# Branch projections of a decoder block: two-sided banks, with gate products and merging on GpSimd

## The chip, the core and the metric

The kernel runs on one core of a Trainium2 chip. The metric is device microseconds of one execution. Engines are named as in the profile: PE is TensorE (PEld its weight loads), ACT is ScalarE, DVE is VectorE, POOL is GpSimd, SP is SyncE, which issues the loads.

## What is computed

One layer of a decoder block over 256 tokens of width 1024, in float32: a SwiGLU feed-forward part, a token mixer, and a second feed-forward part. The mixer has two branches, attention and a gated spatial MLP, each of width 512. Cut to the part that the change touches:

```
y_attn = attn @ w_branch_attn        # (256, 512) @ (512, 1024)
y_gmlp = gm   @ w_branch_gmlp        # (256, 512) @ (512, 1024)
gates  = sigmoid(n @ w_gate + b_gate)             # (256, 2048)
merged = gates[..., :D] * y_attn + gates[..., D:] * y_gmlp
h = h + merged @ w_out                            # (256, 1024) @ (1024, 1024)
```

## The kernel before

Float32 products are made of a high and a low part of each operand: `split` casts a tensor to the matmul type on ACT (the high part, L199) and subtracts it from the original on DVE (the low part, L200). A product is the sum of high by high, high by low and low by high.

**Two ways to multiply.** `mm3` (L183 to L187) issues the three products one by one, each 256 or 512 columns wide. `by_passes` (L166 to L181) works in a bank with two sides: a wide matmul of 512 columns (`mm_high`, L159) multiplies high weights by high and low activations at once and puts them into the two halves of the bank, and a narrow one of 256 columns (`mm_low`, L164) adds low weights by high activations to the second half. The halves are added later by `collect`: ACT copies the second half to a tile `lo` (L192), and DVE adds the first half to it (L196). All wide products but the last stand ahead of the narrow ones.

**Weights.** Units of 1 MB are loaded in halves to seven `raw` buffers by SP, and split into a ring of four `w` buffers. A unit's split can start when PE has read the unit four before it for the last time. The units that matter here are w51 to w54 (branch weights: attention and gMLP for features 0 to 511, then both for 512 to 1023), w55 to w58 (`w_out`) and w59, w60 (the first of the second feed-forward part).

**Order.** PE and SP keep the order of the code. On ACT, DVE and POOL a scheduler sets the order when the program is built, and each engine then works off its row strictly in order. PSUM has eight banks of 128 x 512, given out in turn, so the tile that is allocated eight places later waits for a bank's last reader.

**Around the change.** The loop at L586 goes over eight blocks f of 128 output features. Before it stand 16 gate blocks (`pgate`, by `by_passes`); they leave `gates` in the tile `mix_a`. Each block of the loop takes one bank `pb`: its left half sums the attention branch, its right half the gMLP branch, both by `mm3` with 256 columns, 24 matmuls in all. DVE multiplies each half by its gates straight out of PSUM (L595, L597), adds the two (L599), and `split` makes the block of `mT` (tiles `mg`) of it. Then `down` (L612) multiplies `mT` by `w_out` into four banks `acch`, in 96 matmuls of 512 columns: first the blocks 0 to 3 of `mT` with w55 and w56, for all four banks in turn; then, bank by bank, the blocks 4 to 7 with w57 and w58. After a bank is done DVE adds it to `h` (L286) and multiplies by the norm's gain (L223, `hg`), and PE transposes the result (L216, tile `tr`). The eight transposes of the first token half stand ahead of the last bank's 12 matmuls.

Of the kernel before, what the change touches and what calls it, by code (L numbers as in the profile page):

```python
# [10 lines left out]
F32 = mybir.dt.float32  # L11
# [7 lines left out]
P = 128  # L19
D = 1024  # L20
S = 256
NT = S // P
DFF = 2816
KB = D // P
# [19 lines left out]
def block_kernel(ctx, tc, t, out):  # L44
    nc = tc.nc
# [5 lines left out]
    tmp = ctx.enter_context(tc.tile_pool(name="tmp", bufs=2))  # L51
# [3 lines left out]
    def bank(name):  # L55
        return psum.tile([P, 512], F32, tag="ps", name=name)
# [94 lines left out]
    def unit(i, ahead=PAIRED):  # L151
        split_to(i + 1 + ahead)
        return parts[i]


    def mm_high(ps, st, both, first, last):


        nc.tensor.matmul(ps, st, both.rearrange("p two n -> p (two n)"), start=first, stop=last)  # L159

    def mm_low(ps, st, both):

        n = both.shape[-1]
        nc.tensor.matmul(ps[:, n:], st, both[:, 0, :], start=False, stop=False)  # L164

    def by_passes(sides, ks=range(KB)):  # L166


        for k in ks:
            if k < KB - 1:  # L170
                for ps, of in sides:
                    (sh, _), both = of(k)
                    mm_high(ps, sh, both, k == 0, False)
        for k in ks:
            for ps, of in sides:
                (_, sl), both = of(k)
                mm_low(ps, sl, both)
        if KB - 1 in ks:
            for ps, of in sides:
                (sh, _), both = of(KB - 1)  # L180
                mm_high(ps, sh, both, False, True)  # L181

    def mm3(ps, st, mv_, first, last):  # L183
        (sh, sl), (mh, ml) = st, mv_
        nc.tensor.matmul(ps, sh, mh, start=first, stop=False)  # L185
        nc.tensor.matmul(ps, sh, ml, start=False, stop=False)  # L186
        nc.tensor.matmul(ps, sl, mh, start=False, stop=last)  # L187

    def collect(to, ps, n=1):

        lo = tmp.tile([P, S], F32, tag="lo", name="lo")
        nc.scalar.copy(lo, ps[:, S:])  # L192
        high = ps[:, :S]
        if n > 1:
            high, lo = (x.rearrange("p (n c) -> p n c", n=n) for x in (high, lo))
        nc.vector.tensor_add(to, high, lo)  # L196

    def split(hi, lo, src):
        nc.scalar.copy(hi, src)  # L199
        nc.vector.tensor_sub(lo, src, hi.bitcast(F32))  # L200

    def alloc_T(name, tags):

        return [act.tile([P, 4, 2, S], F32R, tag=tag, name=f"{name}{c}") for c, tag in enumerate(tags)]

    def both_of(nT, k):
        return nT[k // 4][:, k % 4]

    def block_of(nT, k):
        return both_of(nT, k)[:, 0, :], both_of(nT, k)[:, 1, :]  # L210
# [44 lines left out]
    def weights_of(w, nT, blk):  # L255
        c = slice(blk * P, (blk + 1) * P)
        return lambda k: ((w[:, k, 0, c], w[:, k, 1, c]), both_of(nT, k))

    def by_weights(name, i, nT, blk):

        ps, w = bank(name), unit(i, ALONE)
        by_passes([(ps, weights_of(w, nT, blk))])
        return ps

    def by_tokens(name, i, nT, j):

        ps, w = bank(name), unit(i)
        tk = slice(j * P, (j + 1) * P)
        by_passes([(ps, lambda k: (tuple(p[:, tk] for p in block_of(nT, k)), w[:, k]))])
        return ps  # L270
# [66 lines left out]
    def ffn_blocks(i0, aT, nT, rows, name, fs):  # L337
        for f in fs:
            gu = tmp.tile([P, 2, S], F32, tag="gu", name=f"gu{name}{f}")
            w = unit(i0 + f, ALONE)  # L340
            ps = [bank(f"{name}{'gu'[i]}{f}") for i in range(2)]
            by_passes([(ps[i], weights_of(w, nT, i)) for i in range(2)])
            for i in range(2):
                collect(gu[:, i, :], ps[i])
            gate_up(aT, gu, rows, name, f)
# [11 lines left out]
    for k, end in zip(CUTS, CUTS[1:]):  # L357
# [9 lines left out]
        for i in range(2):  # L367
            w = parts[i]
# [6 lines left out]
    for group in ((0, 1), (2,), (3,)):  # L375
        at = [(f, i) for f in group for i in range(2)]
        w = {f: unit(f1 + f, PAIRED if len(group) > 1 else ALONE) for f in group}
        ps = {(f, i): bank(f"f1_{f}{i}") for f, i in at}
        sides = [(ps[f, i], weights_of(w[f], nT, i)) for f, i in at]
# [60 lines left out]
    gates = mix_a[:, :2 * KB, :]  # L440
# [43 lines left out]
    for f in range(4):  # L484
        us = tmp.tile([P, S], F32, tag="us", name=f"uz{f}")
# [5 lines left out]
    for j in range(NT):  # L491
        n = (j + 1) * P
# [3 lines left out]
        for a0 in range(0, HEADS // 2, per):  # L496
# [7 lines left out]
            for two in range(2):  # L504
                ps = pair[two].rearrange("p (a n) -> p a n", a=per)
# [26 lines left out]
    aoT, gmT = alloc_T("ag", ("nC", "nD"))  # L532
# [52 lines left out]
    mT = alloc_T("mg", ("nA", "nB"))  # L585
    for f in range(KB):  # L586
        i = mb + 2 * (f // 4)
        ps = bank(f"pb{f}")
        c = slice(f % 4 * P, (f % 4 + 1) * P)
        for q, bT in enumerate((aoT, gmT)):  # L590
            w = unit(i + q)
            for k in range(4):
                mm3(ps[:, q * S:(q + 1) * S], (w[:, k, 0, c], w[:, k, 1, c]), block_of([bT], k), k == 0, k == 3)
        m0 = tmp.tile([P, S], F32, tag="s", name=f"m0{f}")
        nc.vector.tensor_mul(m0, ps[:, :S], gates[:, f, :])  # L595
        m1 = tmp.tile([P, S], F32, tag="us", name=f"m1{f}")
        nc.vector.tensor_mul(m1, ps[:, S:], gates[:, KB + f, :])  # L597
        m2 = tmp.tile([P, S], F32, tag="a", name=f"m2{f}")
        nc.vector.tensor_add(m2, m0, m1)  # L599
        split(*block_of(mT, f), m2)  # L600

    nT3 = alloc_T("n3", ("nC", "nD"))
# [19 lines left out]
    for j in range(NT):  # L622
        s = tmp.tile([P, UC], F32, tag="s", name=f"s{j}")
# [13 lines left out]
    ms, o = {}, {}  # L637
# [93 lines left out]
```

## Time and profile before

| | us |
|---|---|
| median of three runs (lowest, highest) | 542.71 (542.49, 543.24) |
| the profiled execution | 542.64 |
| its span, first to last instruction | 540.9 |
| PE busy | 532.1 |
| DVE busy | 390.7 |
| ACT busy | 303.2 |
| POOL busy | 10.9 |

The profiled execution is 1.74 us longer than its span, and 0.07 us under the median. The mean granted TensorE clock is 0.997 of full speed. Matmul records overlap, since they are pipelined: what one costs is the distance from its start to the next one's start, not its duration. On ACT and DVE, too, the next instruction starts a little before the one ahead of it has ended.

### The profile page before, as it was taken

The page shows a single profiled execution, that of the slowest core. Times are in us where ns is not written, and L with a number is a line of the kernel's source. Part 1 is how long each engine was busy: PE and PEld are TensorE (multiplying, and loading weights), DVE is VectorE, ACT ScalarE, POOL GpSimd, SP SyncE. Part 2 cuts the span into 40 slices and gives each one's busy share as a digit, 9 for nine tenths or more (in the row PEclk, how much of TensorE's full clock was granted, in tenths as well). Part 3 has the DMA queues.
Part 4 walks back from the last instruction along what each step waited for, and adds up shares of the span by engine and source line. Part 5 has one row for each costly group of instructions (what it writes and reads, how often), then busy time and mean ns, then how long its engine had stood idle before and what let it go on. Part 6 is the DMA issues. An engine that isn't in the chain of part 4 may idle for free.

```text
span 540.9 us, 7971 instructions
## 1 busy us (share of the span) xinstructions
PE 532.1 (98%) x2988; PEld 460.8 (85%) x2988; DVE 390.7 (72%) x632; ACT 303.2 (56%) x541; POOL 10.9 (2%) x23
## 2 busy tenths in 40 slices
PE   8999999999999999999999999999999999999995
PEld 6888888888888888888888998888888888888884
DVE  5989978787434676978896687687787877855324
ACT  6886565565424467457966544575565656543302
POOL 0000000000100010000000000000000000000002
PEclk9999999999999999999999999999999999999998
DMA  8977665657755458464275445466655556465002
GB/s 288 416 276 246 219 214 170 209 180 240 247 194 195 156 196 270 160 226 142 77 215 174 148 154 184 162 210 221 206 180 189 200 180 208 164 219 174 32 0 78
DMA packets 29285, 103.02 MB, mean 190 GB/s; under 512 B 3392, under 2 KB 3904, under 8 KB 29248
## 3 DMA queue, kind: packets, MB, share of 16 engines
q1 hardware_dynamic: 29104, 102.33, 56.6%
q8 instruction: 23, 0.38, 0.3%
q10 hardware_dynamic: 144, 0.20, 0.1%
q14 instruction: 14, 0.11, 0.1%
HBM read 101.46 MB, written 1.05 MB: 190 GB/s over the span
## 4 chain that ended last, share of the span: by engine, by line
PE 96%; DMA 1%; DVE 0%; SPq 0%; ACT 0%; issue 0%; POOLq 0%; DVEq 0%; POOL 0%; ACTq 0%
PE acch L185 9%; PE acch L186 9%; PE acch L187 9%; PE f2u L159 7%; PE f2g L159 7%; PE f1u L159 6%; PE f1g L159 6%; PE pgate L159 6%; PE f2u L164 4%; PE f2g L164 4%; PE f L159 3%; PE f1u L164 3%; PE f1g L164 3%; PE pgate L164 3%; PE pq L159 3%; PE f L164 2%
## 5 line engine op out<-in xcount | busy, mean ns | idle before, releaser
L200 DVE TENSOR_TENSOR w<-raw,w 128x1024 fp32r<-128x1024 f32 x180 | 216.8, 1220 | 57.2 <-ACT w L199 56.5
L199 ACT CAST w<-raw 128x1024 fp32r<-128x1024 f32 x180 | 181.5, 1055 | 59.0 <-PE acch L187 39.6
L159 PE MATMUL f2g<-n,w 128*128 128x512 f32 x160 | 62.7, 392 | 0.0
L159 PE MATMUL f2u<-n,w 128*128 128x512 f32 x160 | 62.6, 392 | 0.0
L159 PE MATMUL f1u<-n,w 128*128 128x512 f32 x144 | 56.4, 391 | 0.0
L159 PE MATMUL f1g<-n,w 128*128 128x512 f32 x144 | 56.4, 391 | 0.0
L164 PE MATMUL f2u<-n,w 128*128 128x256 f32 x160 | 39.3, 283 | 0.0
L164 PE MATMUL f2g<-n,w 128*128 128x256 f32 x160 | 39.1, 283 | 0.0
L164 PE MATMUL f1u<-n,w 128*128 128x256 f32 x144 | 35.3, 284 | 0.0
L164 PE MATMUL f1g<-n,w 128*128 128x256 f32 x144 | 35.2, 283 | 0.0
L159 PEld LDWEIGHTS f2u<-n,w 128*128 128x128 f32 x160 | 30.2, 189 | 5.7
L159 PEld LDWEIGHTS f2g<-n,w 128*128 128x128 f32 x160 | 30.2, 188 | 5.5
L159 PE MATMUL pgate<-n,w 128*128 128x512 f32 x128 | 34.7, 400 | 0.0
L185 PE MATMUL acch<-w,f1h 128*128 128x512 f32 x88 | 34.4, 390 | 0.0
L186 PE MATMUL acch<-w,f1h 128*128 128x512 f32 x88 | 34.3, 390 | 0.0
L187 PE MATMUL acch<-w,f1l 128*128 128x512 f32 x88 | 34.3, 390 | 0.0
L186 PE MATMUL acch<-w,f2h 128*128 128x512 f32 x84 | 32.7, 390 | 0.0
L187 PE MATMUL acch<-w,f2l 128*128 128x512 f32 x84 | 32.7, 390 | 0.0
L185 PE MATMUL acch<-w,f2h 128*128 128x512 f32 x84 | 32.7, 390 | 0.0
L159 PEld LDWEIGHTS f1u<-n,w 128*128 128x128 f32 x144 | 27.1, 189 | 5.1
L159 PEld LDWEIGHTS f1g<-n,w 128*128 128x128 f32 x144 | 27.1, 188 | 5.0
L164 PEld LDWEIGHTS f2u<-n,w 128*128 128x128 f32 x160 | 30.7, 192 | 0.8
(194 smaller groups left out, 989.8 us busy)
## 6 DMA issues: line engine op xcount, KB each, us to landing
raw<-in_f SPq DMA_DIRECT2D x84, 512.0 KB, 4.8
raw<-in_f1d SPq DMA_DIRECT2D x22, 512.0 KB, 4.5
raw<-in_f2d SPq DMA_DIRECT2D x22, 512.0 KB, 4.1
raw<-in_gate SPq DMA_DIRECT2D x16, 512.0 KB, 4.1
raw<-in_qk SPq DMA_DIRECT2D x8, 512.0 KB, 4.9
raw<-in_out SPq DMA_DIRECT2D x8, 512.0 KB, 4.1
raw<-in_v SPq DMA_DIRECT2D x4, 512.0 KB, 4.6
raw<-in_gv SPq DMA_DIRECT2D x4, 512.0 KB, 4.5
```

The source lines that it names most:

```text
L159: nc.tensor.matmul(ps, st, both.rearrange("p two n -> p (two n)"), start=first, stop=last)
L164: nc.tensor.matmul(ps[:, n:], st, both[:, 0, :], start=False, stop=False)
L185: nc.tensor.matmul(ps, sh, mh, start=first, stop=False)
L186: nc.tensor.matmul(ps, sh, ml, start=False, stop=False)
L187: nc.tensor.matmul(ps, sl, mh, start=False, stop=last)
L199: nc.scalar.copy(hi, src)
L200: nc.vector.tensor_sub(lo, src, hi.bitcast(F32))
```

## The change

Each block takes two banks, `pb{f}0` for attention and `pb{f}1` for gMLP. In each, `by_passes` with four k steps sums one branch: three wide matmuls, four narrow ones, the last wide one, the two branches alternating. `collect` (ACT copy, DVE add) brings each bank into an SBUF tile `z`; POOL multiplies each `z` by its gates and adds the two, and `split` follows as before.

```diff
-    def by_passes(sides, ks=range(KB)):
+    def by_passes(sides, ks=range(KB), n=KB):
         for k in ks:
-            if k < KB - 1:
+            if k < n - 1:
                 for ps, of in sides:
                     (sh, _), both = of(k)
                     mm_high(ps, sh, both, k == 0, False)
...
-        if KB - 1 in ks:
+        if n - 1 in ks:
             for ps, of in sides:
-                (sh, _), both = of(KB - 1)
+                (sh, _), both = of(n - 1)
                 mm_high(ps, sh, both, False, True)
...
     for f in range(KB):
         i = mb + 2 * (f // 4)
-        ps = bank(f"pb{f}")
         c = slice(f % 4 * P, (f % 4 + 1) * P)
-        for q, bT in enumerate((aoT, gmT)):
+        pb = [bank(f"pb{f}{q}") for q in range(2)]
+
+        def part_of(q, bT):
             w = unit(i + q)
-            for k in range(4):
-                mm3(ps[:, q * S:(q + 1) * S], (w[:, k, 0, c], w[:, k, 1, c]), block_of([bT], k), k == 0, k == 3)
-        m0 = tmp.tile([P, S], F32, tag="s", name=f"m0{f}")
-        nc.vector.tensor_mul(m0, ps[:, :S], gates[:, f, :])
-        m1 = tmp.tile([P, S], F32, tag="us", name=f"m1{f}")
-        nc.vector.tensor_mul(m1, ps[:, S:], gates[:, KB + f, :])
+            return lambda k: ((w[:, k, 0, c], w[:, k, 1, c]), both_of([bT], k))
+
+        by_passes([(pb[q], part_of(q, bT)) for q, bT in enumerate((aoT, gmT))], range(4), 4)
+        ms = []
+        for q in range(2):
+            z = tmp.tile([P, S], F32, tag=("s", "us")[q], name=f"z{q}{f}")
+            collect(z, pb[q])
+            nc.gpsimd.tensor_mul(z, z, gates[:, q * KB + f, :])
+            ms.append(z)
         m2 = tmp.tile([P, S], F32, tag="a", name=f"m2{f}")
-        nc.vector.tensor_add(m2, m0, m1)
+        nc.gpsimd.tensor_add(m2, *ms)
         split(*block_of(mT, f), m2)
```

Three places in the engines' rows show what moves. On PE, block 4 before: the attention half of its 24 matmuls (`ag0` holds the attention branch, w53 its weights).

```order
L185 MATMUL pb4_3241<-ag0_2536,w53_3038 128x256
L186 MATMUL pb4_3241<-ag0_2536,w53_3038 128x256
L187 MATMUL pb4_3241<-ag0_2536,w53_3038 128x256
L185 MATMUL pb4_3241<-ag0_2536,w53_3038 128x256
L186 MATMUL pb4_3241<-ag0_2536,w53_3038 128x256
L187 MATMUL pb4_3241<-ag0_2536,w53_3038 128x256
...
L187 MATMUL pb4_3241<-ag0_2536,w53_3038 128x256
L185 MATMUL pb4_3241<-ag1_2537,w54_3113 128x256
```

The same place of PE in the changed kernel: the wide ones of both branches, then narrow ones, then the last two wide ones.

```order
L159 MATMUL pb40_3237<-ag0_2536,w53_3038 128x512
L159 MATMUL pb41_3238<-ag1_2537,w54_3102 128x512
L159 MATMUL pb40_3237<-ag0_2536,w53_3038 128x512
...
L159 MATMUL pb41_3238<-ag1_2537,w54_3102 128x512
L164 MATMUL pb40_3237<-ag0_2536,w53_3038 128x256
L164 MATMUL pb41_3238<-ag1_2537,w54_3102 128x256
...
L164 MATMUL pb41_3238<-ag1_2537,w54_3102 128x256
L159 MATMUL pb40_3237<-ag0_2536,w53_3038 128x512
L159 MATMUL pb41_3238<-ag1_2537,w54_3102 128x512
```

A block has 8 wide and 8 narrow matmuls now, in place of 24 narrow ones, and both branches end together. On ACT, before, the rows from the cast of block 2 (`m22`) to the first cast of w58:

```order
L199 CAST mg0_3098<-m22_3204 128x256
L199 CAST w55_3242<-raw55_0_2897 128x1024
L199 CAST w55_3242<-raw55_1_2967 128x1024
L199 CAST w56_3263<-raw56_0_2971 128x1024
L199 CAST w56_3263<-raw56_1_3041 128x1024
L199 CAST mg0_3098<-m23_3237 128x256
L199 CAST mg1_3099<-m24_3288 128x256
L199 CAST mg1_3099<-m25_3321 128x256
L199 CAST w57_3397<-raw57_0_3045 128x1024
L199 CAST mg1_3099<-m26_3354 128x256
L199 CAST w57_3397<-raw57_1_3116 128x1024
L199 CAST w58_3430<-raw58_0_3120 128x1024
```

The changed kernel on ACT, from the copies of block 3 to the cast of block 4 (`pb40` is block 4, attention):

```order
L192 COPY lo_3224<-pb30_3205 128x256
L192 COPY lo_3229<-pb31_3206 128x256
L199 CAST w55_3239<-raw55_0_2897 128x1024
L199 CAST w55_3239<-raw55_1_2967 128x1024
L199 CAST mg0_3098<-m23_3233 128x256
L199 CAST w56_3248<-raw56_0_2971 128x1024
L199 CAST w56_3248<-raw56_1_3041 128x1024
L192 COPY lo_3274<-pb40_3237 128x256
L192 COPY lo_3279<-pb41_3238 128x256
L192 COPY lo_3306<-pb50_3287 128x256
L192 COPY lo_3311<-pb51_3288 128x256
L199 CAST mg1_3099<-m24_3283 128x256
```

And the rows of ACT that follow these, up to the casts of w58:

```order
L192 COPY lo_3338<-pb60_3319 128x256
L192 COPY lo_3343<-pb61_3320 128x256
L199 CAST mg1_3099<-m25_3315 128x256
L199 CAST mg1_3099<-m26_3347 128x256
L192 COPY lo_3370<-pb70_3351 128x256
L192 COPY lo_3375<-pb71_3352 128x256
L199 CAST w57_3389<-raw57_0_3045 128x1024
L199 CAST w57_3389<-raw57_1_3105 128x1024
L199 CAST mg1_3099<-m27_3379 128x256
L199 CAST w58_3422<-raw58_0_3109 128x1024
L199 CAST w58_3422<-raw58_1_3242 128x1024
```

Sixteen copies are new on ACT, the cast of block 3 now stands between w55 and w56 with the copies of blocks 4 and 5 behind w56, and the casts of w57 stand behind those of blocks 5 and 6 and the copies of block 7. POOL's row gets 24 instructions, three for each block in order. On DVE the two adds of each block take the place of the two products and the sum, and the subtractions of w56 stand ahead of the adds of block 4.

## Rows read from the trace of the kernel before

**Rows 1.** Page, part 1: busy time, share of the span, instructions.
```profile
PE 532.1 (98%) x2988; PEld 460.8 (85%) x2988; DVE 390.7 (72%) x632; ACT 303.2 (56%) x541; POOL 10.9 (2%) x23
```

**Rows 2.** Waits of PE in the whole span: total us, times, longest.
```profile
PE warm L93 <- DVE zeros L90: 1.2, 1, 1.2
PE f L159 <- ACT w L199: 1.1, 2, 0.8
```

**Rows 3.** Chain that ended last, in order of time: start us, us, what.
```profile
290.69 1.84 PE pgate L159 x8
292.53 0.95 PE pgate L164 x8
```

**Rows 4.** Timeline of PE: start, us, what.
```profile
304.56 0.28 PE L185 MATMUL pb<-ag,w 128*128 128x256 f32 x1
...
327.60 0.40 PE L185 MATMUL acch<-w,mg 128*128 128x512 f32 x1
...
338.50 0.39 PE L185 MATMUL acch<-w,mg 128*128 128x512 f32 x1
...
346.67 1.03 PE L216 MATMUL tr<-ident,hg 128*128 128x128 f32 x8
...
371.82 0.28 PE L164 MATMUL f2g<-n,w 128*128 128x256 f32 x1
...
377.39 0.28 PE L164 MATMUL f2g<-n,w 128*128 128x256 f32 x1
```

**Rows 5.** Timeline of ACT, with idle time before and its releaser.
```profile
304.81 0.37 ACT L192 COPY lo<-pgate 128x256 f32<-128x256 f32 x1 [1.33 <-PE pgate L159]
305.08 2.00 ACT L199 CAST w<-raw 128x1024 fp32r<-128x1024 f32 x2
...
314.64 0.41 ACT L199 CAST mg<-m 128x256 fp32r<-128x256 f32 x1 [2.47 <-DVE m L599]
314.96 3.89 ACT L199 CAST w<-raw 128x1024 fp32r<-128x1024 f32 x4
```

**Rows 6.** Timeline of DVE.
```profile
306.16 2.36 DVE L200 TENSOR_TENSOR w<-raw,w 128x1024 fp32r<-128x1024 f32 x2
308.44 0.42 DVE L595 TENSOR_TENSOR m<-pb,mix_a 128x256 f32<-128x256 f32 x1
...
319.31 1.22 DVE L200 TENSOR_TENSOR w<-raw,w 128x1024 fp32r<-128x1024 f32 x1
320.44 0.42 DVE L200 TENSOR_TENSOR mg<-m,mg 128x256 fp32r<-128x256 f32 x1
...
332.56 1.22 DVE L200 TENSOR_TENSOR w<-raw,w 128x1024 fp32r<-128x1024 f32 x1
...
342.11 0.69 DVE L286 SCALAR_TENSOR_TENSOR h<-acch,h 128x512 f32<-128x512 f32 x1
...
344.87 0.69 DVE L223 TENSOR_TENSOR hg<-h,gain 128x512 f32<-128x512 f32 x1
```

**Rows 7.** Groups of POOL: count, busy us, mean ns, idle before.
```profile
L664 POOL TENSOR_TENSOR o<-o,rstd 128x512 f32<-128x512 f32 x1 | 1.0, 1041 | 0.1
L656 POOL TENSOR_TENSOR ms<-ss,eps 128x1 f32<-128x1 f32 x2 | 0.4, 190 | 173.2 <-ACT sq L652 173.2
```

**Rows 8.** Instructions on the tile rstd: least, median, greatest ns.
```profile
L243 POOL TENSOR_TENSOR rstd<-ms,nhalf x6: 548/548/1463, 26.8 to 354.7; 128x1 f32<-128x1 f32 x6
```

**Rows 9.** Timelines of DVE and POOL around 194 us.
```profile
194.31 0.15 DVE L241 TENSOR_SCALAR ms<-ms 128x1 f32<-128x1 f32 x1
194.38 1.21 DVE L200 TENSOR_TENSOR w<-raw,w 128x1024 fp32r<-128x1024 f32 x1
...
194.54 1.46 POOL L243 TENSOR_TENSOR rstd<-ms,nhalf 128x1 f32<-128x1 f32 x1 [7.98 <-DVE ms L241]
```

**Rows 10.** Busy us (x instructions) by stretch: PE, PEld, DVE, ACT, POOL; clock, DMA.
```profile
304.50:327.60 23.10, 23.10 (x194) 23.06 (x194) 17.93 (x36) 10.12 (x16) 0.00 (x0) 1.00 0.44 149
```

## Prediction

> **What bounds the kernel now.** I read the page's busy times first: PE is busy for 98% of the span [rows 1]. Its list of waits says how much of the rest a change could win: 2.3 us in all, both waits in the first stage, none after it [rows 2]. So PE is the bound from then on, and a change pays what it takes off PE's own row, as long as no other engine becomes late. The busy table by stretch shows the stage: in 23.1 us PE never pauses, DVE works 17.9 us, ACT 10.1, POOL not at all [rows 10]. The timeline of PE gives its ends: the first branch matmul starts at 304.56 and the first of `w_out` at 327.60, which is 23.04 us for 192 matmuls, 0.120 each [rows 4].
>
> **PE's term.** The matmuls that replace them are in the trace already. In a gate block, eight wide ones take 1.84 us (0.230 each) and eight narrow ones 0.95 [rows 3]: 2.79 for a block of the new form, 22.32 for eight. The blocks of the second feed-forward part alternate two banks as the new ones do, with twice the k steps: one starts its narrow matmuls at 371.82, the next at 377.39 [rows 4], so half of one is 2.785, eight 22.28. I take 2.785: the stage is 0.76 us shorter. The bounds are a wide one at 0.227, as in `w_out` (48 from 327.60 to 338.50 [rows 4]), with a narrow one at 0.119, and a wide one at twice a narrow one's 0.120, which gains nothing: 0.9 to 0 us.
>
> **What is added, and its cover.** Sixteen ACT copies of 0.37 us; per block, two DVE adds of 0.42 replace two products and a sum of the same length; 24 POOL instructions. By busy time all this fits: ACT comes to 16 of 22.3 us, DVE to 15. But a block now passes ACT, DVE, POOL and ACT again before its copy is done, and ACT's row is strict: a cast that waits for POOL holds up the copies and the weight casts behind it. So I walked the rows of the four engines in order, each instruction starting when its engine is free and what it reads is there, with these durations. ACT starts the next instruction 0.27 after a copy (304.81 to 305.08), 0.32 after a cast of a block (314.64 to 314.96), 0.95 after a weight cast (four in 3.89) [rows 5]. DVE goes on 1.13 after a weight subtraction (319.31 to 320.44) [rows 6], 0.33 after an add. An engine starts 0.03 after the end of what it waits for, POOL after 0.08 (194.46 to 194.54 [rows 9]); I take 0.12. Walked in the same way, the rows of before give 342.06 for the first `h` add, which the trace has at 342.11 [rows 6], so the method holds to a tenth.
>
> **POOL's price.** No row has this instruction. The same operation takes 1.04 us on 512 columns and 0.19 on one [rows 7]. The straight line between gives 0.615 for 256; half of the long one is 0.52, the floor, and the whole 1.04 is the ceiling. With a fixed part somewhat under 0.19 it is 0.59. I take 0.60, since the same operation at twice the width is the nearest row; its second operand was one column repeated, which the new ones are not, and that is the weak point.
>
> **DVE and POOL in each other's way.** The small power on POOL takes 0.55 us, once 1.46 [rows 8]. That once it started at 194.54 while DVE subtracted a weight half, from 194.38 to 195.59, and it ended at 196.00, 0.41 after DVE [rows 9]: it did most of its work behind the subtraction. The Trainium skill says why, in "SBUF — State Buffer", section "Who interferes with whom": a DVE instruction with both inputs in SBUF and a GpSimd one that reads SBUF exclude each other; this row agrees. In the walk POOL's reading, from 0.14 after its start, and DVE's weight and block subtractions exclude each other, and whoever starts first goes first. The new adds have one input in PSUM and are left free.
>
> **The walk.** Block f is ready at 304.56 + 2.785(f+1) + 0.17, block 0 at 307.51. DVE is busy with w54 until 308.44, as before [rows 6]. From then on the copies of one block, its adds, three POOL steps and its cast take about 1.37 + 3 x 0.60 = 3.17 us, more than PE's 2.785; ACT's order lets no copy of blocks 1 to 3 pass the cast ahead of it. So ACT reaches block 3's copies at 317.49, 1.6 us after the block. Behind them stand w55's casts, block 3's cast (321.21, its sum having waited for a subtraction of w55), w56's casts, and only then block 4's copies (323.43).
> - First deadline: `down` takes the banks of blocks 4 and 5, as the eighth tiles after them; before, those of blocks 0 to 3, long free. PE arrives at 304.56 + 22.28 = 326.84; DVE has emptied the first bank at 325.29. In hand: 1.5 us.
> - Second: ACT waits for POOL with the casts of blocks 4, 5 and 6 (327.26, 329.29, 331.32), then copies block 7 and casts w57 from 332.18, waits for block 7 (335.36), and casts w58. DVE ends w58's second half at 339.11, where before it was done at 333.78 [rows 6]. PE needs it after 57 matmuls of `down`: 326.84 + 57 x 0.227 = 339.8. In hand: 0.7.
> - Third: w59 and w60 occupy DVE until 343.6; then come two `h` adds with two gains, done at 346.27. Before, the last of these ended at 345.56, for transposes at 346.67 [rows 4, 6]. Now the four transposes that need it are due at 346.40. In hand: 0.1.
>
> At 0.60 no wait reaches PE. Later weights have several us in hand.
>
> **The sum.** 542.64 for the profiled execution (540.9 of span and 1.74 around it) - 0.76 = 541.9; it lay 0.07 under the median of 542.71, so the median comes to 542.0. That is 0.14%, inside the 0.2% that a measurement of this kernel can tell from no change.
>
> **What POOL's price does to it.** With the exclusion, 0.615 makes the last transposes wait 0.25: -0.5 us. At 0.65 w58 is 0.5 late too: +0.3. At 0.67 `down` begins to wait for its first bank, which pushes DVE's subtractions behind POOL's reads once more, and w58 is 2.8 late: +3.0. At 0.70: +3.6; at 0.73: +4.3; at the ceiling of 1.04: +11.7. Without the exclusion: -0.76 up to 0.68, +0.1 at 0.73, +7.6 at 1.04.
>
> **The rivals.**
> - *POOL is slower on two full tiles, and the mixer waits for it* (slower). The place is the start of `down` and w58; it decides from 0.66 us per POOL instruction on. For it: the row of 0.60 rests on a repeated column, and the walk's margins are tenths. Against: an instruction would have to be a tenth over the line between the two rows. At 0.67 to 0.74 it gives +3.0 to +4.5, 545.6 to 547.1.
> - The Trainium skill's "GPSIMD Engine Reference", section 3.1, speaks for this rival: 4497 ns for such an addition of 2048 columns, about 2.6 cycles an element. My estimate from that page, its slope on the 0.19 us of one column, is 0.73 us for 256 columns, and the sum would be 546.9. The row of 512 columns goes against it: that rate would have made it 1.27, not 1.04; but no row has two full operands.
> - *The copies never matter, and the wide matmuls run as in* `w_out`, with later waits on PE's sequencer gone too: over 1.09 us of gain, under 541.6. For it only the spread of the runs and the 0.9 above; PE has no other idle time to give back here [rows 2, 10].
> - *Nothing happens*: the new matmuls cost as much per column as the old ones, because the banks alternate; 542.7. The feed-forward blocks alternate and have the low price [rows 4].
>
> **How the numbers follow.** No or hardly a wait on PE, 541.7 to 542.5: 0.46, with 0.08 of that for gains that measure as more than 0.2%. A short wait or no gain, to 543.7: 0.17. The mixer waits for POOL, 543.8 to 546.6: 0.27; above that 0.10. So faster 0.08, same 0.55, slower 0.37. The predicted time is that of the first case. The range leaves out the tenth above, and something below 541.7: 541.7 to 546.6. The likeliest case alone: 541.7 to 542.5.
>
> **What the profile after would show.** PE's term: 128 `pb` matmuls, a block each 2.79 us, 22.3 from the first to `down`. POOL's price: the spacing of its 24 instructions; 0.60 is right, 0.70 is the rival. The lag: ACT's copies of block 4 at about 323.4, after w56's casts. Margins: no wait of PE on DVE between 326 and 350; the rival shows a gap before the first `acch` matmul, another before w58, and a third before the transposes. Exclusion: POOL's sum of block 3 stretched or late by a subtraction of w55. I would be wrong through POOL's duration first, and through the walk's margins second.

## The result, and the profile after

The changed kernel takes 548.24 us (median of 5 runs, 547.86 to 548.79); the kernel before, on the same chip, 542.98 (5 runs, 542.49 to 543.78). The ratio is 1.0098, with an interval of 1.0087 to 1.0109: 5.3 us slower (4.7 to 5.9). The prediction was 542.0, with a range of 541.7 to 546.6. The profiled execution took 548.13, with a span of 546.4, which is 5.5 over the span before.

The page's busy times of the changed kernel, and its chain that ended last by engine, to be read beside [rows 1]:

```profile
PE 535.1 (98%) x2924; PEld 459.1 (84%) x2924; DVE 388.8 (71%) x624; ACT 307.5 (56%) x557; POOL 33.0 (6%) x47
PE 90%; POOL 3%; DVE 2%; issue 2%; ACT 1%; DMA 1%; POOLq 0%; DVEq 0%; ACTq 0%
```

The shares alone mislead. PE is still busy for 98%, POOL for only 6%. But POOL now has 3% of the chain, 16 us: it has become part of what sets the end. The waits of PE of the changed kernel, which answer to [rows 2], say where that happens (total us, times, longest):

```profile
PE acch L185 <- ACT w L199: 1.2, 1, 1.2
PE warm L93 <- DVE zeros L90: 1.2, 1, 1.2
PE acch L185 <- DVE z L196: 0.9, 1, 0.9
PE acch L186 <- DVE w L200: 0.8, 1, 0.8
PE f L159 <- ACT w L199: 0.6, 1, 0.6
```

Three waits of the matmuls of `down` are new. The timeline of PE in the changed kernel puts them in time, as in [rows 4]:

```profile
304.93 1.54 PE L159 MATMUL pb<-ag,w 128*128 128x512 f32 x6
...
326.82 0.63 PE L159 MATMUL pb<-ag,w 128*128 128x512 f32 x2
328.31 0.50 PE L185 MATMUL acch<-w,mg 128*128 128x512 f32 x1 [0.86 <-DVE z L196]
...
340.62 0.40 PE L187 MATMUL acch<-w,mg 128*128 128x512 f32 x1
342.26 0.50 PE L185 MATMUL acch<-w,mg 128*128 128x512 f32 x1 [1.24 <-ACT w L199]
343.52 0.60 PE L186 MATMUL acch<-w,mg 128*128 128x512 f32 x1 [0.76 <-DVE w L200]
343.92 0.63 PE L187 MATMUL acch<-w,mg 128*128 128x512 f32 x1
...
347.29 0.39 PE L186 MATMUL acch<-w,mg 128*128 128x512 f32 x1
...
351.86 1.03 PE L216 MATMUL tr<-ident,hg 128*128 128x128 f32 x8
```

Read the distances of starts. From the first branch matmul to the first of `down` it is 23.38 us, against 23.04 before: PE's own work is shorter, and the wait for the bank costs 1.03. From there to the transposes it is 23.55, against 19.07: 4.48 more. Of these, 1.41 and 1.03 are the two stops for the last unit of `w_out` (1.64 and 1.26 less the 0.23 that a matmul takes anyhow). Another 1.73 is not a wait at all: from 343.52 to 347.29 nine matmuls start 0.42 us apart on average, which makes 3.77 us, where 9 x 0.227 is 2.04. The remaining 0.3 are matmuls next to a stop that stand up to 0.34 apart instead of 0.23. Together the two stretches are 4.8 us longer; 0.37 more lay ahead of the stage in this execution, 0.3 behind it.

The busy table of the changed kernel by stretch says what the slow matmuls are (columns as in [rows 10]):

```profile
304.90:327.30 22.40, 22.40 (x129) 19.47 (x127) 12.22 (x20) 10.90 (x22) 10.57 (x12) 1.00 0.33 111
328.40:340.60 12.20, 12.20 (x53) 9.89 (x54) 6.61 (x12) 4.85 (x11) 10.58 (x12) 1.00 0.31 100
340.60:343.50 2.90, 0.92 (x3) 0.19 (x1) 1.69 (x3) 2.65 (x4) 0.22 (x1) 1.00 0.80 249
343.50:347.30 3.80, 3.78 (x10) 2.75 (x11) 3.80 (x4) 3.44 (x4) 0.00 (x0) 0.55 0.60 179
```

The granted clock is 1.00 up to 343.50 and 0.55 in the 3.8 us behind it: TensorE ran nearly all of them at the lower of its two levels, 1.2 GHz. Ahead of that PE had worked 0.92 of 2.90 us. The single stop at 327 to 328 did not lower it: the row behind it has 1.00. All this is read from the one profiled execution. The mean granted clock of the five executions is 0.993 (the profiled one), 0.995, 0.996, 0.993 and 0.996, where the 56 executions of the kernel before in the experiments have 0.996 to 0.999; whether all five had the slow stretch is not shown.

Why POOL is in the chain stands in its groups in the changed kernel, which answer to [rows 7]:

```profile
L600 POOL TENSOR_TENSOR z<-z,mix_a 128x256 f32<-128x256 f32 x16 | 13.9, 890 | 92.7 <-DVE z L196 92.7
L603 POOL TENSOR_TENSOR m<-z,z 128x256 f32<-128x256 f32 x8 | 7.6, 951 | 0.6
```

The two means hide two cases. The least, median and greatest ns of the same two groups:

```profile
L600 POOL TENSOR_TENSOR z<-z,mix_a x16: 730/740/1775, 309.3 to 337.4; 128x256 f32<-128x256 f32 x16
L603 POOL TENSOR_TENSOR m<-z,z x8: 732/736/1601, 310.8 to 339.2; 128x256 f32<-128x256 f32 x8
```

An instruction that nothing holds up costs about 0.735 us (medians of 740 and 736 ns), not 0.60, and some last 1.6 to 1.8. The timeline of POOL in the changed kernel shows which:

```profile
312.88 1.43 POOL L600 TENSOR_TENSOR z<-z,mix_a 128x256 f32<-128x256 f32 x2 [1.31 <-DVE z L196]
...
316.43 1.43 POOL L600 TENSOR_TENSOR z<-z,mix_a 128x256 f32<-128x256 f32 x2 [1.31 <-DVE z L196]
...
319.98 2.47 POOL L600 TENSOR_TENSOR z<-z,mix_a 128x256 f32<-128x256 f32 x2 [1.31 <-DVE z L196]
322.53 1.60 POOL L603 TENSOR_TENSOR m<-z,z 128x256 f32<-128x256 f32 x1
```

The timeline of DVE has the first of these rows beside the last two, and the second where block 4's first add stands:

```profile
320.63 2.90 DVE L200 TENSOR_TENSOR w<-raw,w 128x1024 fp32r<-128x1024 f32 x2 [0.40 <-ACT w L199]
...
327.84 0.75 DVE L196 TENSOR_TENSOR z<-pb,lo 128x256 f32<-128x256 f32 x2
```

POOL's loop comes round every 3.55 us (312.88 to 316.43), while PE makes a block in 2.79. And block 3's second product and its sum, which meet the two subtractions of w55, take 1.0 and 0.9 us longer than their fellows; the subtractions take 2.90 instead of the 2.36 of a pair left alone [rows 6].

How that reaches PE is read on ACT, which works off its row strictly in order. Its timeline in the changed kernel:

```profile
318.71 0.41 ACT L199 CAST mg<-m 128x256 fp32r<-128x256 f32 x1 [2.60 <-POOL m L603]
...
324.17 0.41 ACT L199 CAST mg<-m 128x256 fp32r<-128x256 f32 x1 [2.62 <-POOL m L603]
324.48 2.00 ACT L199 CAST w<-raw 128x1024 fp32r<-128x1024 f32 x2
326.37 0.64 ACT L192 COPY lo<-pb 128x256 f32<-128x256 f32 x2
...
340.85 0.40 ACT L199 CAST mg<-m 128x256 fp32r<-128x256 f32 x1 [2.62 <-POOL m L603]
341.17 5.78 ACT L199 CAST w<-raw 128x1024 fp32r<-128x1024 f32 x6
```

Block 4 is copied at 326.37 (the walk had 323.4 at a price of 0.60), and DVE adds it from 327.84, behind the subtractions of w56; so the bank that `down` wants first comes free too late, and its first matmul starts at 328.31. Block 7's cast waits until 340.85, and the casts of w58, the first of the six at 341.17, stand behind it: PE wants that unit at 340.9. Both stops there are for the first half of w58, at the 55th and 56th matmul of `down`; the walk had set its deadline by the second half, after 57.

### The profile page after: what moved, and what is told of

Read it like the earlier page. It is cut to its first block, busy times and chain, and to the rows that moved or that the text cites. A ratio compares the mean times of both kernels' runs of the same rounds, so it can differ in the third digit from the quotient of the medians.

```text
span 546.4 us, 7894 instructions
## 1 busy us (share of the span) xinstructions
PE 535.1 (98%) x2924; PEld 459.1 (84%) x2924; DVE 388.8 (71%) x624; ACT 307.5 (56%) x557; POOL 33.0 (6%) x47
## 4 chain that ended last, share of the span: by engine, by line
PE 90%; POOL 3%; DVE 2%; issue 2%; ACT 1%; DMA 1%; POOLq 0%; DVEq 0%; ACTq 0%
PE acch L186 8%; PE acch L187 8%; PE acch L185 8%; PE f2u L159 7%; PE f2g L159 7%; PE f1u L159 6%; PE f1g L159 6%; PE pgate L159 6%; PE f L159 4%; PE f2u L164 4%; PE f2g L164 3%; PE f1u L164 3%; PE f1g L164 3%; PE pgate L164 3%; PE pq L159 3%; PE f L164 2%
```

## The experiments

All are compared with runs of the kernel before on the same chip: median 542.74 for the matmuls alone, for products and sum on VectorE, for one column repeated in all three, and for GpSimd's part alone; 542.92 for one input tile on VectorE; 542.72 for the other four.

| | us | ratio to before |
|---|---|---|
| the matmuls alone | 541.99 | 0.9986 (0.9977 to 0.9995) |
| products and sum on VectorE | 541.72 | 0.9980 (0.9972 to 0.9989) |
| one column repeated, all three | 542.53 | 0.9998 (0.9989 to 1.0007) |
| products repeated | 543.54 | 1.0013 (1.0004 to 1.0022) |
| sum repeated | 546.83 | 1.0070 (1.0056 to 1.0084) |
| GpSimd's part alone | 547.37 | 1.0086 (1.0072 to 1.0100) |
| last unit early | 546.70 | 1.0070 (1.0056 to 1.0083) |
| only the sum on GpSimd | 541.97 | 0.9984 (0.9975 to 0.9993) |
| one input tile on VectorE | 545.21 | 1.0041 (1.0026 to 1.0055) |

The theory: the matmuls win their 0.76 us, and the 24 GpSimd instructions make ACT late for two deadlines of `down`, because each costs 0.735 us and because GpSimd and VectorE's subtractions with two input tiles keep each other out (called the exclusion below). The first rival: the loss lies in the matmuls, the second bank or ACT's copies. The second: the exclusion plays no part.

### The two halves of the change apart

The kernel before with the new matmuls; VectorE multiplies straight from the first half of each bank, and the second halves are left out:

```diff
-        nc.vector.tensor_mul(m0, ps[:, :S], gates[:, f, :])
+        nc.vector.tensor_mul(m0, pb[0][:, :S], gates[:, f, :])
...
-        nc.vector.tensor_mul(m1, ps[:, S:], gates[:, KB + f, :])
+        nc.vector.tensor_mul(m1, pb[1][:, :S], gates[:, KB + f, :])
```

> The new matmuls in two banks, with DVE multiplying the first half of each bank straight out of PSUM and adding the two, as before; the second halves are left out, and with them the copies, the adds and GpSimd. Theory 1 (GpSimd's price at 0.735 us and its exclusion with DVE stall the mixer): PE's term alone is left, so 0.76 us faster than before, 22.3 us from the first branch matmul to the first of w_out, no wait of PE after the first stage. Theory 2 (the new order of matmuls or the two banks make PE or the banks late): still slower than before by several us.

Measured: 0.75 us faster. Its timeline of PE:

```profile
304.64 1.54 PE L159 MATMUL pb<-ag,w 128*128 128x512 f32 x6
...
327.00 0.39 PE L185 MATMUL acch<-w,mg 128*128 128x512 f32 x1
...
346.06 1.03 PE L216 MATMUL tr<-ident,hg 128*128 128x128 f32 x8
```

22.36 us from the first branch matmul to `down`, 19.06 from there to the transposes: PE's term stands, and in this stage no wait takes anything back.

The other half alone: the matmuls of before in one bank, which ACT copies for POOL:

```diff
-        nc.vector.tensor_mul(m0, ps[:, :S], gates[:, f, :])
...
-        nc.vector.tensor_mul(m1, ps[:, S:], gates[:, KB + f, :])
+            nc.scalar.copy(z, ps[:, q * S:(q + 1) * S])
+            nc.gpsimd.tensor_mul(z, z, gates[:, q * KB + f, :])
...
-        nc.vector.tensor_add(m2, m0, m1)
+        nc.gpsimd.tensor_add(m2, *ms)
```

> The kernel before with its 24 matmuls a block in one bank, but ACT copies both halves of the bank to SBUF and GpSimd multiplies and adds; no DVE adds. Theory 1: the stall comes with GpSimd, without the new matmuls: the walk gives a wait of about 3.2 us before the second half of w58 and 0.6 at the transposes, together 3.8 us slower than before, and up to 2 more if the clock falls behind the gap as in the changed kernel. Theory 2: no slower than before by more than the copies, that is within 0.5 us.

Measured: 4.6 us slower, most of the loss without one new matmul. Its waits of PE:

```profile
PE acch L185 <- ACT w L199: 2.0, 1, 2.0
PE acch L186 <- DVE w L200: 0.8, 1, 0.8
```

And its busy table behind the second of them:

```profile
343.50:347.30 3.80, 3.47 (x9) 2.76 (x10) 3.80 (x5) 2.81 (x3) 0.00 (x0) 0.55 0.57 186
```

The same unit is late, and the clock falls again behind the stops, for as long. The bank of `down` is in time here: its first matmul comes 23.04 us after the first branch matmul, as before, since a block takes one bank.

### The same copies and adds, but on VectorE

```diff
-            nc.gpsimd.tensor_mul(z, z, gates[:, q * KB + f, :])
+            nc.vector.tensor_mul(z, z, gates[:, q * KB + f, :])
...
-        nc.gpsimd.tensor_add(m2, *ms)
+        nc.vector.tensor_add(m2, *ms)
```

> The changed kernel with products and sum on DVE; all else as changed. Theory 1: the walk through the rows, with 0.42 us for each of the three, has DVE done with the second half of w58 at 335.5 and no wait of PE: 0.76 us faster than before, about 542.1. Theory 2 (the additional pass through ACT copies and DVE adds is what comes too late, whoever multiplies): slower than before by 2 us or more, with a gap of PE before w58.

Measured: 1.02 us faster, the best of all kernels here. The second bank, the copies on ACT and the adds cost nothing here, which speaks against the first rival. One caution: the scheduler gives ACT another row in this kernel, where the first copy of block 1 (309.84 us) stands ahead of the cast of block 0 (310.11). That the row alone isn't the cause is shown below by the kernels that keep the changed kernel's row. VectorE has the room: in its busy table it works 20.2 of the 22.4 us, and PE never pauses.

```profile
304.20:326.60 22.40, 22.40 (x130) 19.71 (x129) 20.18 (x44) 12.56 (x27) 0.00 (x0) 1.00 0.47 147
```

With the products on VectorE and only the sum on GpSimd:

```diff
-            nc.gpsimd.tensor_mul(z, z, gates[:, q * KB + f, :])
+            nc.vector.tensor_mul(z, z, gates[:, q * KB + f, :])
```

> The products on VectorE, only the sum of each block on GpSimd, at 0.735 us. A block's chain then takes 0.3 us more than with all of it on VectorE, and no wait reaches TensorE by the walk: -0.8 us like the version with all of it on VectorE (-1.0 measured there). If one GpSimd instruction a block is enough to disturb VectorE's subtractions by the exclusion (0.6 us each time), some tenths come back at most, -0.5. If it is any use of GpSimd that costs, it lies above 0.

Measured: 0.75 us faster. Its sums last 0.73 to 0.79, but one 1.59, and no wait reaches PE. One GpSimd step a block is free here, so it is not any use of the engine that costs. ACT's row is again another than that of the changed kernel.

### The price, in four steps

Four kernels, the changed one among them, have one and the same order of instructions on ACT, DVE and POOL in this stage, and differ in GpSimd's second operands alone. First, all three instructions of a block with a repeated column:

```diff
-            nc.gpsimd.tensor_mul(z, z, gates[:, q * KB + f, :])
+            nc.gpsimd.tensor_mul(z, z, gates[:, q * KB + f, 0:1].to_broadcast([P, S]))
...
-        nc.gpsimd.tensor_add(m2, *ms)
+        nc.gpsimd.tensor_add(m2, ms[0], ms[1][:, 0:1].to_broadcast([P, S]))
```

> The changed kernel, with every row of instructions the same, but the second operand of each GpSimd product and of the sum is one column repeated 256 times, so the values are others. Theory 1, and the reason given for its wrong price (a repeated column is cheaper than a full tile): GpSimd takes 0.59 to 0.615 us for one that no DVE subtraction holds up, and the walk gives 0.76 to 0.5 us faster than before. If the pattern of the operand does not matter: 0.735 us each and 5 us slower than before, as the changed kernel.

Measured: 0.21 us faster, which the interval doesn't tell from no change. The least, median and greatest ns of its products and sums:

```profile
L600 POOL TENSOR_TENSOR z<-z,mix_a x16: 612/613/841, 309.0 to 333.3; 128x256 f32<-128x256 f32 x16
L603 POOL TENSOR_TENSOR m<-z,z x8: 612/612/1474, 310.2 to 334.0; 128x256 f32<-128x256 f32 x8
```

Two rows of ACT's timeline, the copies of block 4 and the cast of block 7:

```profile
323.49 0.64 ACT L192 COPY lo<-pb 128x256 f32<-128x256 f32 x2
...
335.52 0.41 ACT L199 CAST mg<-m 128x256 fp32r<-128x256 f32 x1 [1.20 <-POOL m L603]
```

And its first transposes on PE's timeline:

```profile
345.99 1.26 PE L216 MATMUL tr<-ident,hg 128*128 128x128 f32 x8
```

The price is that of the straight line in the prediction, 0.615, to 3 ns, and the time that the prediction gave for it, -0.5, is 0.3 off. The walk at 0.60 had these two rows of ACT at 323.43 and 335.36. The eight transposes take 1.26 instead of 1.03: the third deadline is missed by 0.23, where the walk had 0.25. The changed kernel's own row of instructions loses nothing at this price; so its loss comes with the price.

Then only the sum repeated (the second edit alone), and only the products (the first alone):

> Leaves out the true sum: the second operand of GpSimd's sum is one column repeated, the two products keep their full tiles; the order of all instructions is that of the changed kernel. Two thirds of GpSimd's instructions then cost 0.735 us, a third 0.613: 0.69 on average. If the loss is a matter of deadlines that GpSimd's steps miss together with the exclusion between VectorE's two-input subtractions and GpSimd, the walk gives a wait of 0.6 at the first matmul of down and of 2.9 at its last unit, +3.4 us, and up to 1.7 more if the clock falls again behind the second: +3.4 to +5.1. If the two engines did not exclude each other, the rows alone give -0.8. If the loss grew evenly with the price (from -0.2 at 0.613 to +5.3 at 0.735), it would be two thirds of the way: +3.4.

> Leaves out the true products: their second operand is one column repeated, the sum keeps two full tiles; same order of instructions. The average price is 0.65 us. Deadlines with the exclusion: the first bank is in time, the last unit of down comes 0.6 late, the transposes 0.6: +0.4 us, and at most some tenths from the clock, since the gaps are short. Without the exclusion: -0.8. Growing evenly with the price: a third of the way from -0.2 to +5.3, +1.6.

Measured: with the sum repeated, an average price of 0.69, 4.1 us slower; with the products repeated, 0.65, 0.8 slower. PE's timeline with the sum repeated:

```profile
328.15 0.50 PE L185 MATMUL acch<-w,mg 128*128 128x512 f32 x1 [0.39 <-DVE z L196]
...
341.63 0.50 PE L185 MATMUL acch<-w,mg 128*128 128x512 f32 x1 [0.94 <-ACT w L199]
...
342.89 0.50 PE L186 MATMUL acch<-w,mg 128*128 128x512 f32 x1 [0.76 <-DVE w L200]
...
351.32 0.63 PE L216 MATMUL tr<-ident,hg 128*128 128x128 f32 x4 [0.66 <-DVE hg L223]
```

With the products repeated, `down` starts without a wait, and the only one of PE that the view marks in this stretch is that of the transposes. The 0.6 us that were expected at the last unit did not come: there two matmuls stand 0.45 apart (340.64 to 341.09) instead of 0.23.

```profile
348.38 0.63 PE L216 MATMUL tr<-ident,hg 128*128 128x128 f32 x4 [0.66 <-DVE hg L223]
```

At 0.613, 0.65, 0.69 and 0.735 us the change measures -0.2, +0.8, +4.1 and +5.3; the walk gives -0.5, +0.4, +3.4 and +4.3. It is a step between 0.65 and 0.69, where the bank and w58 begin to be late, and no even growth: that would have been +1.6 at 0.65, where the interval is 0.2 to 1.2. At 0.69 even growth would give +3.4, which the interval (3.0 to 4.6) does not exclude. Without the exclusion the walk gives -0.8 for both of the middle ones, and both were slower than before, which speaks against the second rival.

### The exclusion, taken away

The low parts of the four units of `w_out` are made by an instruction with one input tile, of nearly the same length (1.28 us for 1.22):

```diff
-                split(w[:, sl, 0, :], w[:, sl, 1, :], raws.pop((i, hf)))
+                src = raws.pop((i, hf))
+                if mo <= i < mo + 4:
+                    hi, lo = w[:, sl, 0, :], w[:, sl, 1, :]
+                    nc.scalar.copy(hi, src)
+                    sink = small.tile([P, 1], F32, tag="sink", name=f"sink{i}{hf}")
+                    nc.vector.tensor_scalar(lo, src, hi.bitcast(F32)[:, 0, 0:1], None, op0=ALU.mult, op1=ALU.add, accum_out=sink)
+                else:
+                    split(w[:, sl, 0, :], w[:, sl, 1, :], src)
```

> Leaves out the low parts of the four units of w_out: VectorE writes a multiple of the raw weights there, with one input tile instead of two, so it no longer does a two-input subtraction while GpSimd works, save those of the blocks. If GpSimd's steps of 1.60 to 1.78 us in the changed kernel are waits for the two-input subtractions, they are gone beside the weights' instructions: all 24 of GpSimd's stay under 1.0 us, and by the walk the first matmul of down doesn't wait and the last unit waits 1.9, +1.8 us, with at most some tenths of clock (the low parts also take other places in VectorE's row, which is why it does not fall to the +0.2 of the walk without exclusion). If the long steps come from something else that stands there (ScalarE's casts, the DMA), they stay at 1.6 or more and the time at about +5.3.

Measured: 2.3 us slower, 3 less than the changed kernel. Its products and sums on GpSimd, in least, median and greatest ns:

```profile
L607 POOL TENSOR_TENSOR z<-z,mix_a x16: 732/740/921, 308.8 to 336.3; 128x256 f32<-128x256 f32 x16
L610 POOL TENSOR_TENSOR m<-z,z x8: 737/740/745, 310.3 to 337.1; 128x256 f32<-128x256 f32 x8
```

One meeting of the two engines, GpSimd's sum of block 3 on its timeline:

```profile
320.99 0.74 POOL L610 TENSOR_TENSOR m<-z,z 128x256 f32<-128x256 f32 x1
```

And VectorE's timeline beside it:

```profile
320.12 1.28 DVE L153 TENSOR_SCALAR_CACHE_REDUCE w<-raw,w 128x1024 fp32r<-128x1024 f32 x1 [0.40 <-ACT w L151]
...
321.33 1.27 DVE L153 TENSOR_SCALAR_CACHE_REDUCE w<-raw,w 128x1024 fp32r<-128x1024 f32 x1
```

Both engines work in the same microseconds and neither gets longer: the steps of 1.6 us were waits for the subtractions. The operation is another one too, so this run alone doesn't separate the second input from the operation. At the same 0.735 us the bank is in time now: `down` starts at 326.75, 22.36 after the first branch matmul. What is left of the loss are w58 (stops of 0.82 and 0.24) and the transposes (0.66). The expectation's +1.8 is 0.5 short but within the interval (1.4 to 3.0). One caution: the scheduler also put the copies of block 6 behind the cast of block 5, so the 3 us are not the exclusion's alone; what this order costs or saves is not measured.

### The last unit, out of ACT's queue

```diff
+        if f == KB - 1:
+            split_to(mo + 4)
         m2 = tmp.tile([P, S], F32, tag="a", name=f"m2{f}")
```

> The changed kernel with one edit: the casts and subtractions of the last unit of down (w58) are asked for before the cast of the mixer's last block, so ScalarE's row no longer holds them behind GpSimd. If the second pair of gaps comes from that row, w58 is in time and only block 7's own merged tile and the start of down wait: the walk leaves 1.1 us at the start and 1.8 at the end of down instead of 3.4, +3.1 us, and less than +0.8 us of clock: +2.5 to +3.9. If the late thing were GpSimd's chain itself, nothing changes: +5.3.

Measured: 4.0 us slower (interval 3.0 to 4.5, expected up to 3.9), 1.3 less than the changed kernel's 5.3. PE waits 0.71 and 0.17 in the last unit in place of 1.24 and 0.76. Its busy table behind these:

```profile
343.50:347.30 3.80, 3.69 (x16) 2.96 (x17) 3.80 (x6) 2.08 (x3) 0.00 (x0) 1.00 0.82 240
```

And the second four of its transposes on PE's timeline:

```profile
351.24 0.63 PE L216 MATMUL tr<-ident,hg 128*128 128x128 f32 x4 [0.70 <-DVE hg L223]
```

The clock stays at 1.00, and the transposes wait, as they did not in the changed kernel. So the slow stretch comes with the longer stops ahead of it, and it covers the third deadline: while PE ran at the lower level, VectorE caught up. Taking the wait of 0.70 off its 1.73 us, I estimate that about 1.0 was a loss of its own in the profiled execution.

## Why the prediction was wrong

- **PE's term was right**: -0.76 us predicted, -0.75 measured alone, with 22.36 us for 22.28 from the first branch matmul to `down`.
- **POOL's price failed.** The step is "I take 0.60, since the same operation at twice the width is the nearest row", which it itself called the weak point. The operation is 0.735 with two full tiles and 0.613 with one column repeated, in the same place of the same program. So the lines of the prediction on 0.615 describe the repeated column, and a block's chain takes 3.55 us where 3.17 were reckoned. By an estimate from the 0.19 us of one column, two full tiles cost 2.14 ns a further column, and the row of 1.04 us, with a repeated one, 1.67.
- The rule that spoke against the change was right: the estimate from the Trainium skill's "GPSIMD Engine Reference", section 3.1, was 0.73, and the trace agrees with 0.735. I set it aside for the row of 512 columns, though that row's second operand was one column repeated.
- **The exclusion was right**: block 3's sum is stretched by a subtraction of w55, as said (1.60 against 0.735), and in the run with one input tile on VectorE the same sum lasts 0.74. The section "Who interferes with whom" of the Trainium skill's "SBUF — State Buffer" says that a VectorE instruction with two SBUF inputs contends with a GpSimd one that reads SBUF, and that one with at most one such input, outside the two-port modes, does not; the traces agree.
- **The walk was right in its mechanism**: it named the start of `down` and w58 as the places and 0.66 as the price from which they decide, and four prices in place of one confirm the step. That its +4.3 for 0.73 comes near the measured 5.3 is in part luck, for two errors work against each other. Its stops in the last unit were too long: 3.4 us at 0.735, where 2.4 were measured. And **the clock was missing**: the table of prices counted stops as stops alone, and in the profiled execution the two in the last unit were followed by 1.73 us of loss at the lower level, which covered the third wait of 0.7.
- **The third deadline** was missed by 0.23 us at 0.613 and by 0.66 at 0.65 and 0.69, much as the walk had it. At 0.735 the transposes did not wait, because the slow stretch came ahead of them.
- **The chances**: all that is slower had 0.37, but what came true, a mixer that waits and a time above 546.6, had 0.10 of it. The range was cut at 546.6, though the rival's own working went to 547.1.

## What to carry to other kernels

Take the price of an instruction from a row with the same kind of operands, not only the same operation: one repeated column in place of a second tile made a GpSimd instruction 17% cheaper here. Where the margins of the engines behind it are tenths of a microsecond, a price doesn't cost in proportion but by a step: find the price at which the walk breaks, and count what the clock takes behind the stops. Here the chain through one more engine was free with one step of it, while three made the kernel 5.3 us slower; the version with all of it on VectorE has the lowest median, 541.72 us.

## What the runs showed of the hardware

- In the profiled executions, two stops of 1.24 and 0.76 us within 2.9 us were followed by 3.8 us at a granted clock of 0.55, and so were stops of 1.97 and 0.76 in the run of GpSimd's part alone. Stops of 0.94, 0.76 and 0.17 with the sum repeated left it at 1.00, as did those of 0.71 and 0.17 with the last unit early and a single one of 0.86. It can differ between executions of one kernel: with the sum repeated their mean granted clock is 0.999 (the profiled one), 0.996, 0.999 and 0.993, and 0.993 is that of the changed kernel's profiled execution. What decides is not settled by these runs.
- GpSimd and a two-input subtraction of VectorE delay each other: 0.74 becomes 1.6 to 1.8 us, a pair of subtractions 2.36 becomes 2.90. Beside an instruction of VectorE with one input tile, GpSimd's steps stay at 0.73 to 0.75, and VectorE's at 1.28.
- The start of the mixer's matmuls lay between 304.28 and 305.40 in the profiles, whatever the kernel; this comes from the stages ahead, so differences of a few tenths between two spans say nothing of the change. The 0.27 us by which VectorE's version beats the matmuls alone is not told from nothing either: their intervals overlap.
